# Layer 0's modulation and early-shift sums: VectorE's 32x32 block transposes and one small product each in place of ScalarE's copy and four TensorE transposes

## The chip, the core and the metric

The kernel runs on one core of a Trainium2 chip. Five engines work in parallel, each through its own instructions in program order: TensorE (PE; its weight loads are listed apart as PEld), VectorE (DVE), ScalarE (ACT), GpSimd (POOL) and SyncE (SP), whose queue issues the DMAs. The metric is the device time of one execution in microseconds (us), as the median of the runs.

## The reference

Two layers over 256 latent and 256 context tokens of width 2048. Layer 0 mixes tokens by centred pooling in four channel groups; layer 1 by neighbourhood attention. Each is followed by a gated MLP with a width-3 convolution (inner width 5504). Cut to what bears on the change:

```python
silu_c, silu_cc = jax.nn.silu(c), jax.nn.silu(c_ctx)
for i in range(DEPTH):                                  # DEPTH = 2
    ml = (silu_c @ w_mod[i] + b_mod[i]).reshape(B, 6, 1, D)     # latent: 6 chunks of D
    mc = (silu_cc @ w_mod[i] + b_mod[i]).reshape(6, 1, 1, D)    # context, same weights
    a_lat = modulate(rms_norm(h, norm1_g[i]), ml[:, 0], ml[:, 1])
    a_ctx = modulate(rms_norm(hc, norm1_g[i]), mc[0], mc[1])
    ...                                                 # i == 0: y = pool_mix(a)
    h = h + ml[:, 2] * y_lat
    h = h + ml[:, 5] * conv_ffn(modulate(rms_norm(h, norm2_g[i]), ml[:, 3], ml[:, 4]),
                                ffn_w_gate[i], ffn_w_up[i], ffn_conv_w[i], ffn_conv_b[i], ffn_w_down[i])
```

`modulate(x, shift, scale)` is `x * (1 + scale) + shift`. The context stream goes through the same steps with `mc`.

## The kernel before

Activations lie with channels on the partitions: 16 blocks of 128 channels, 256 latent and 256 context columns. Products with the large weights run as three TensorE passes over rounded high and low parts (high x high, high x low, low x high); ScalarE casts the high part of a weight tile and VectorE subtracts it to get the low part (`split`, lines 143 and 145; tiles such as `wcu_4h` and `wcu_4l`). The tiles of the high parts come from a pool of three buffers, so the cast of a new tile also waits until TensorE has read the old one.

Layer 0's modulation is 24 chunks of 512 channels: chunk 4w+g is part w of the six (shift, scale, gate, then the MLP's three) in channel group g. Generator `mod_pe` makes one chunk in 16 small TensorE products (line 193, tile `mod`), each with 32 columns of weights at one of four column positions of the array; a product is float32 and shows as two matmuls in the trace. Its result, 128 partitions by 512, holds the two streams in a few rows, and in partial sums over four row blocks. To get channels onto the partitions, ScalarE copies the PSUM bank to `modev` (line 198), TensorE transposes it in four pieces into `modt` (line 203), VectorE reduces over the row blocks (`by_row`, line 205) and adds the bias (`finish_mod`, line 181; for scales, line 183 follows). Only one PSUM bank, tag `m`, serves the `mod` tiles, so a chunk's first product waits until the chunk before it was read out.

The order of the chunks is per group g: g, 4+g, 8+g, 16+g, 12+g, then 20 to 23. `need(n)` steps this row of generators from within the code of the mixer and of `partial`.

The pooling mixer works per channel group: `mixer(g)` normalises and modulates (`py`, line 453; `pad` on ScalarE), sums windows by doubling (`ws`, line 461, VectorE), divides (`pf` on GpSimd, line 466), subtracts (line 467) and splits into high and low (`ph`), for four blocks; then a 512x512 product `pm` with the split weights `wph`, `wpl`; `gsc` and `gbi` come from the gate chunk 8+g. Group g+1's mixer is interleaved with `partial(g, ...)`, which runs the first eight column blocks of the MLP's gate and up products over group g's channels (`cg`, `cu`, lines 545 to 547) as soon as those channels are ready.

The MLP's shift term goes through the same weights: `partial` has small products `pwg` and `pwu` (line 528), also 32 columns wide, 16 times in all (four groups, two halves, gate and up). They are turned like the modulation: ScalarE's copy `peg`, `peu` (line 532), four transposes `ptg`, `ptu` (line 561), a reduce, and for g > 0 an add into `wsh` (lines 564 to 569).

Layer 1's modulation is made on VectorE instead (line 241) and already ends in a block transpose (line 251) and a product with `quad`, a matrix of ones where partition numbers agree modulo 32 (`quarter_sum`, line 165).

The order of the instructions on each engine comes from a scheduler that takes its priorities from the order of the code; `tc.high_priority()` raises what stands under it. The text of the kernel alone does not give the order.

Of the kernel before, what the change touches and what calls it, by code (L numbers as in the profile page):

```python
# [10 lines left out]
F32 = mybir.dt.float32  # L11
F32R = mybir.dt.float32r
AF = mybir.ActivationFunctionType
ALU = mybir.AluOpType
AX = mybir.AxisListType
PSUM = bass.MemoryType.PSUM

P = 128
# [39 lines left out]
def kernel(ctx: ExitStack, tc: tile.TileContext, xT, cxT, wmod, wg, wu, wd, wp,  # L58
                         wq, wv, wo, vec, cc, rope, inv, strips, out):
    nc = tc.nc  # L60
    main = ctx.enter_context(tc.tile_pool(name="main", bufs=1))
# [7 lines left out]
    def bank(tag, name):  # L69

        if tag == "d" and nbank[0] is not None:
            nbank[0] += 1
            if nbank[0] % 4 == 0:
                tag = "m"
        return pp.tile([P, 512], F32, tag=tag, bufs={"gu": 4, "d": 3, "m": 1}[tag], name=name)

    def flat(a):
        return a.rearrange("p s t -> p (s t)")
# [5 lines left out]
    def V(name):  # L84
        a, b = _OFF[name]
        return vt[:, a:b]
# [5 lines left out]
    ident = main.tile([P, P], F32, name="ident")  # L92
# [60 lines left out]
    modT = {}  # L153

    both = (0, 1)

    def by_row(ps):

        return ps.rearrange("p (i j c) -> p i c j", i=4, j=4)[:, :, 0:2, :]

    def quarter_sum(x, n, name):


        ps = bank("d", f"{name}s")
        nc.tensor.matmul(ps[:, : 16 * n].rearrange("p (k s) -> p k s", s=n), quad, x, start=True, stop=True)
        v = ps[:, : 16 * n].rearrange("p (i b s) -> p i b s", b=4, s=n)
        return [v[32 * b : 32 * b + 32, :, b, :] for b in range(4)]

    def finish_mod(l, ch, streams, src):

        mt = src[0] if len(src) == 1 else main.tile([P, 4, 2], F32, name=f"modT{l}_{ch}")
        n = len(streams)
        which, q = divmod(ch, 4)

        def dup(name, a):
            return V(name)[:, a : a + 8].rearrange("p (i s) -> p i s", s=2)[:, :, 0:n]

        bias = dup(f"bm_{l}", 8 * ch)
        for b, v in enumerate(src):
            own = slice(32 * b, 32 * b + 32) if len(src) > 1 else slice(0, P)  # L180
            nc.vector.tensor_tensor(mt[own, :, 0:n], v, bias[own], op=ALU.add)
        if which in (1, 4):
            nc.vector.scalar_tensor_tensor(mt[:, :, 0:n], mt[:, :, 0:n], 1.0, dup(f"g{1 if which == 1 else 2}_{l}", 8 * q),
                                           op0=ALU.add, op1=ALU.mult)
        modT[l, ch] = mt

    def mod_pe(l, ch, sc, pool):

        ps = bank("m", f"mod{l}_{ch}")
        for g in range(4):  # L190
            ts = load(lambda a, b: wmod[l, ch, g, :, a:b], 2048, f"wm{l}_{ch}_{g}")
            for j in range(4):
                nc.tensor.matmul(ps[32 * j : 32 * j + 32, :], sc[:, 4 * g + j, :],  # L193
                                 ts[j // 2][0][:, 512 * (j % 2) : 512 * (j % 2) + 512],
                                 start=(g == 0), stop=(g == 3), tile_position=(0, 32 * j))
            if g == 3:
                ev = pool.tile([P, 512], F32, tag="t2", name=f"modev{l}_{ch}")
                nc.scalar.copy(ev, ps)
            yield
        with tc.high_priority():  # L200
            p2 = bank("d", f"modt{l}_{ch}")
            for i in range(4):
                nc.tensor.transpose(p2[:, P * i : P * i + P], ev[:, P * i : P * i + P], ident)
        r = main.tile([P, 4, 2], F32, name=f"modT{l}_{ch}")
        nc.vector.tensor_reduce(out=r, in_=by_row(p2), axis=AX.X, op=ALU.add)
        finish_mod(l, ch, both, [r])

    def mod_pairs(todo, ring):

# [113 lines left out]
    with ExitStack() as ph0:  # L323
        p0 = ph0.enter_context(tc.tile_pool(name="p0", bufs=1, reuse_waits="tile"))
        f0 = ph0.enter_context(tc.tile_pool(name="f0", bufs=6, reuse_waits="tile"))
# [18 lines left out]
        wsh = p0.tile([P, 2, NS, 2], F32, name="wsh")  # L344
# [41 lines left out]
        with ExitStack() as phs:  # L386
# [16 lines left out]
            for j in range(2):  # L403
                t = st.tile([P, 2, WP], F32, bufs=1, name=f"pad{j}")
# [3 lines left out]
            for j in range(2):  # L408
                t = st.tile([P, 4, 32], F32, bufs=1, name=f"sh{j}")
# [100 lines left out]
            def partial(g, sh, between):  # L510

                step = 0
                for fa in range(0, NS, 4):
                    for q, (nm, wsrc) in enumerate((("g", wg), ("u", wu))):
                        ts = load(lambda a, b: wsrc[0, fa + a // 512 : fa + b // 512, :, 512 * g : 512 * g + 512]
                                  .rearrange("f p c -> p f c"), 2048, f"wc{nm}{g}_{fa}")
                        parts = split(ts, f"wc{nm}{g}_{fa}")
                        for j in range(4):
                            f = fa + j
                            between(2 * step)  # L520
                            if j == (3 if fa == 0 and q == 0 else 0):
                                need(20 * g + 21)
                                assert g in READY
                                pw = bank("d", f"pw{nm}{g}_{fa}")
                                for i in range(4):
                                    for jj, (t, n) in enumerate(ts):
                                        t3 = t.rearrange("p (f c) -> p f c", c=512)
                                        nc.tensor.matmul(pw[32 * i : 32 * i + 32, 256 * jj : 256 * jj + 256], sh[:, i, :],
                                                         t3[:, :, P * i : P * i + P], start=True, stop=True,
                                                         tile_position=(0, 32 * i))  # L530
                                ev = f0.tile([P, 512], F32, tag="t2", name=f"pe{nm}{g}_{fa}")
                                nc.scalar.copy(ev, pw)
                            if f >= NC:
                                if g == 0:
                                    HELD[f, q] = bank("gu", f"c{nm}_{f}")
                                ps = HELD[f, q]
                                first, final = g == 0, g == 3
                            else:
                                ps = bank("d", f"c{nm}{g}_{f}")
                                first = final = True  # L540
                            hi, lo = parts[j // 2]
                            for i in range(4):
                                c = 512 * (j % 2) + P * i
                                xh, xl = flat(A[4 * g + i][:, 0]), flat(A[4 * g + i][:, 1])
                                nc.tensor.matmul(ps, hi[:, c : c + P], xh, start=(first and i == 0), stop=False)
                                nc.tensor.matmul(ps, hi[:, c : c + P], xl, start=False, stop=False)
                                nc.tensor.matmul(ps, lo[:, c : c + P], xh, start=False, stop=(final and i == 3))
                                if i == 1:
                                    between(2 * step + 1)
                            step += 1  # L550
                            if f >= NC:
                                continue
                            if g == 0:
                                if q == 0:
                                    PART[f] = act_tile(f"part{f}", F32)
                                nc.scalar.copy(PART[f][:, q], ps)
                            else:
                                nc.vector.tensor_tensor(PART[f][:, q], PART[f][:, q], ps, op=ALU.add)
                        p2 = bank("d", f"pt{nm}{g}_{fa}")
                        for i in range(4):  # L560
                            nc.tensor.transpose(p2[:, P * i : P * i + P], ev[:, P * i : P * i + P], ident)
                        w_ = wsh[:, q, fa : fa + 4, :]
                        if g == 0:
                            nc.vector.tensor_reduce(out=w_, in_=by_row(p2), axis=AX.X, op=ALU.add)
                            continue
                        t_ = f0.tile([P, 512], F32, tag="t2", name=f"pu{nm}{g}_{fa}")[:, 0:8]
                        t_ = t_.rearrange("p (f s) -> p f s", s=2)
                        nc.vector.tensor_reduce(out=t_, in_=by_row(p2), axis=AX.X, op=ALU.add)
                        nc.vector.tensor_tensor(w_, w_, t_, op=ALU.add)
            lend(range(4, KT))  # L570
            mix = mixer(0)
            for n in STEPS:
# [141 lines left out]
    with ExitStack() as ph2:  # L714
# [136 lines left out]
        for j, (a, b) in enumerate(((0, 4), (4, 6), (6, 8), (8, 12), (12, 16))):  # L851
            v = hl[:, a:b, :]
# [379 lines left out]
```

## Time and profile before

| | before |
|---|---|
| median of three runs | 3102.25 us (3098.42 to 3103.55) |
| profiled execution | 3103.48 us |
| its span | 3101.7 us |
| granted TensorE clock, mean | 0.993 |
| TensorE busy | 3030.0 us (98%) |
| VectorE busy | 1932.6 us (62%) |
| ScalarE busy | 1373.2 us (44%) |
| GpSimd busy | 826.1 us (27%) |

The profiled execution is one run; 1.78 us of its time lie outside the span. The work around the change lies in about the first 475 us. Shares over the whole span are means over stages with different limits.

### The profile page before, as it was taken

What the parts mean: (1) busy time and instruction counts of PE and PEld (TensorE: products, weight loads), DVE (VectorE), ACT (ScalarE), POOL (GpSimd) and SP (SyncE); (2) the same over time, 40 slices, a digit from 0 to 9 for tenths busy, and PEclk for the clock granted to TensorE, in tenths of its full rate; (3) what the DMA queues carried; (4) which work ended last, traced back from release to release, by engine and by line L of the source; (5) the groups of instructions that cost most, each with busy time, mean ns of one, the idle gap of its engine ahead of it and who ended that gap; (6) DMA issues with size and microseconds to landing.
All of it is one profiled execution on the core that took longest, in us unless ns stands there. A gap on an engine that the chain in (4) does not pass through costs nothing.

```text
span 3101.7 us, 40819 instructions
## 1 busy us (share of the span) xinstructions
PE 3030.0 (98%) x15082; PEld 2414.3 (78%) x15082; DVE 1932.6 (62%) x2748; ACT 1373.2 (44%) x2219; POOL 826.1 (27%) x823
## 2 busy tenths in 40 slices
PE   6999899999999999999999999999999999999998
PEld 2565558888888888888888788878788888888887
DVE  4445674285765848567485665564777666666666
ACT  3333454333233332323334444343545666656665
POOL 2011213213031230302213000000002466556665
PEclk9999999999999999999999999999999999999999
DMA  9978573264846657475573333332345565555563
GB/s 376 333 271 306 177 246 102 89 217 149 251 141 206 198 162 247 133 225 171 182 226 118 102 113 106 102 114 96 111 153 179 177 196 188 192 189 185 179 195 117
DMA packets 177927, 559.70 MB, mean 180 GB/s; under 512 B 17600, under 2 KB 22208, under 8 KB 177728
## 3 DMA queue, kind: packets, MB, share of 16 engines
q1 hardware_dynamic: 177728, 557.10, 55.0%
q8 instruction: 119, 1.95, 0.3%
q14 instruction: 80, 0.66, 0.1%
HBM read 554.93 MB, written 2.10 MB: 180 GB/s over the span
## 4 chain that ended last, share of the span: by engine, by line
PE 94%; DMA 2%; DVE 2%; POOL 1%; ACT 1%; issue 0%; SPq 0%; DVEq 0%; ACTq 0%; POOLq 0%
PE g L766 5%; PE u L766 5%; PE d L657 5%; PE d L659 5%; PE d L658 5%; PE d L813 4%; PE u L631 4%; PE u L632 4%; PE u L633 4%; PE g L631 4%; PE g L633 4%; PE g L632 4%; PE mod L193 3%; PE u L769 3%; PE g L769 3%; PE d L817 2%
## 5 line engine op out<-in xcount | busy, mean ns | idle before, releaser
L670 POOL TENSOR_TENSOR hl<-hl,dy 128x256 f32<-128x256 f32 x160 | 149.0, 931 | 958.6 <-ACT dy L669 957.3
L828 POOL TENSOR_TENSOR hl<-hl,dy 128x256 f32<-128x256 f32 x320 | 331.5, 1069 | 188.4 <-ACT dy L826 186.1
L241 DVE SCALAR_TENSOR_TENSOR macc<-wm,sc,macc 128x512 f32<-128x512 f32 (+1 forms) x360 | 325.2, 935 | 68.6 <-DMA wm<-wmod 67.6
L669 ACT ACTIVATE dy<-d,modT 128x256 f32<-128x256 f32 x320 | 133.5, 470 | 196.8 <-PE d L659 195.5
L193 PE MATMUL mod<-wm,sc 128*32 128x512 f32 x768 | 134.6, 618 | 26.6 <-DMA wm<-wmod 26.5
L670 POOL TENSOR_TENSOR hc<-hc,dy 128x256 f32<-128x256 f32 x160 | 126.0, 787 | 0.0
L145 DVE TENSOR_TENSOR wd_2l<-wd,wd_2h 128x1024 fp32r<-128x1024 f32 (+1 forms) x44 | 53.9, 1229 | 112.8 <-ACT wd_2h L143 112.8
L826 ACT ACTIVATE dy<-d,modT 128x512 f32<-128x512 f32 x160 | 104.4, 683 | 42.7 <-PE d L817 41.2
L915 POOL TENSOR_TENSOR rk<-rk,rp 128x256 f32<-128x256 f32 x16 | 13.2, 826 | 365.4 <-DVE rk L914 309.8
L145 DVE TENSOR_TENSOR wd_3l<-wd,wd_3h 128x1024 fp32r<-128x1024 f32 (+1 forms) x44 | 52.0, 1202 | 80.6 <-ACT wd_3h L143 80.6
L145 DVE TENSOR_TENSOR wd_1l<-wd,wd_1h 128x1024 fp32r<-128x1024 f32 (+1 forms) x44 | 53.7, 1224 | 58.6 <-ACT wd_1h L143 58.6
L466 POOL TENSOR_TENSOR pf<-ws,inv 128x256 f32<-128x256 f32 x32 | 27.7, 886 | 222.4 <-DVE ws L461 154.7
L193 PEld LDWEIGHTS mod<-wm,sc 128*32 128x32 f32 x768 | 23.6, 110 | 81.0 <-issue 59.4
L143 ACT CAST wd_1h<-wd 128x1024 fp32r<-128x1024 f32 (+1 forms) x44 | 45.2, 1029 | 79.8 <-PE u L632 50.6
L145 DVE TENSOR_TENSOR wd_0l<-wd,wd_0h 128x1024 fp32r<-128x1024 f32 (+1 forms) x44 | 54.6, 1247 | 40.7 <-ACT wd_0h L143 40.6
L1004 ACT ACTIVATE sb<-sb,nm 128x512 f32<-128x512 f32 x64 | 46.1, 721 | 64.4 <-DVE nm L1000 63.2
L143 ACT CAST wd_0h<-wd 128x1024 fp32r<-128x1024 f32 (+1 forms) x44 | 45.3, 1031 | 57.9 <-PE u L766 29.1
L792 DVE TENSOR_TENSOR actb<-sgb,actb 128x256 fp32r<-128x256 f32 x43 | 52.3, 1216 | 27.0 <-ACT actb L791 27.0
L657 PE MATMUL d<-act,wd_2h 128*128 128x512 f32 x172 | 68.0, 395 | 0.0
L658 PE MATMUL d<-act,wd_2h 128*128 128x512 f32 x172 | 67.9, 395 | 0.0
L657 PE MATMUL d<-act,wd_3h 128*128 128x512 f32 x172 | 67.9, 395 | 0.0
L657 PE MATMUL d<-act,wd_0h 128*128 128x512 f32 x172 | 67.9, 395 | 0.0
(1752 smaller groups left out, 9286.1 us busy)
## 6 DMA issues: line engine op xcount, KB each, us to landing
wm<-wmod SPq DMA_DIRECT2D x384, 512.0 KB, 6.1
wd<-wd SPq DMA_DIRECT2D x168, 512.0 KB, 4.4
wg<-wg SPq DMA_DIRECT2D x156, 512.0 KB, 4.6
wu<-wu SPq DMA_DIRECT2D x156, 512.0 KB, 4.5
wv<-wv SPq DMA_DIRECT2D x32, 512.0 KB, 3.9
wk<-wq SPq DMA_DIRECT2D x32, 512.0 KB, 4.0
wq<-wq SPq DMA_DIRECT2D x32, 512.0 KB, 3.7
wo<-wo SPq DMA_DIRECT2D x32, 512.0 KB, 4.4
```

What stands on the lines that cost most here:

```text
L145: eng.tensor_tensor(lo[:, :n], t[:, :n], hi[:, :n].bitcast(F32), op=ALU.subtract)
L193: nc.tensor.matmul(ps[32 * j : 32 * j + 32, :], sc[:, 4 * g + j, :], ts[j // 2][0][:, 512 * (j % 2) : 512 * (j % 2) + 512], start=(g == 0) ...
L241: nc.vector.scalar_tensor_tensor(acc[s], v, sc2[:, k, s : s + 1], acc[s], op0=ALU.mult, op1=ALU.add)
L631: nc.tensor.matmul(ps, hi[:, c : c + P], xh, start=(k == 0), stop=False)
L632: nc.tensor.matmul(ps, hi[:, c : c + P], xl, start=False, stop=False)
L633: nc.tensor.matmul(ps, lo[:, c : c + P], xh, start=False, stop=(k == KT - 1))
L657: nc.tensor.matmul(ps, hi[:, o : o + P], xh, start=(i == 0), stop=False)
L658: nc.tensor.matmul(ps, hi[:, o : o + P], xl, start=False, stop=False)
L670: nc.gpsimd.tensor_tensor(h_of(s)[:, k, :], h_of(s)[:, k, :], y[:, s], op=ALU.add)
L766: nc.tensor.matmul(ps, hi[:, c : c + P], flat(B[k]), start=(k == 0), stop=False)
L769: nc.tensor.matmul(ps[:, T:], lo[:, c : c + P], B[k][:, 0], start=False, stop=(k == KT - 1))
L828: nc.gpsimd.tensor_tensor(hl[:, k, :], hl[:, k, :], y[:, q], op=ALU.add)
```

## The change

For all 24 chunks of layer 0's modulation and for the 16 shift sums, `turned` takes the place of ScalarE's copy: VectorE transposes the PSUM bank in blocks of 32x32 into a tile in SBUF. `quarter_sum` then takes the place of the four TensorE transposes and of the reduce: one float32 product of `quad` with a strided 32 columns of that tile. Its result lies in four quarters of 32 partitions, so `finish_mod` makes four adds in place of one, and a shift sum ends in four copies (g = 0) or four adds.

```diff
-    def by_row(ps):
-        return ps.rearrange("p (i j c) -> p i c j", i=4, j=4)[:, :, 0:2, :]
+    def turned(ps, pool, name):
+        t = pool.tile([P, 512], F32, tag="t2", name=name)
+        nc.vector.transpose(t, ps)
+        return t.rearrange("p (k r) -> p k r", r=32)[:, :, 0:2]
...
             if g == 3:
-                ev = pool.tile([P, 512], F32, tag="t2", name=f"modev{l}_{ch}")
-                nc.scalar.copy(ev, ps)
+                x = turned(ps, pool, f"modev{l}_{ch}")
             yield
         with tc.high_priority():
-            p2 = bank("d", f"modt{l}_{ch}")
-            for i in range(4):
-                nc.tensor.transpose(p2[:, P * i : P * i + P], ev[:, P * i : P * i + P], ident)
-        r = main.tile([P, 4, 2], F32, name=f"modT{l}_{ch}")
-        nc.vector.tensor_reduce(out=r, in_=by_row(p2), axis=AX.X, op=ALU.add)
-        finish_mod(l, ch, both, [r])
+            v = quarter_sum(x, 2, f"modt{l}_{ch}")
+        finish_mod(l, ch, both, v)
...
-                                ev = f0.tile([P, 512], F32, tag="t2", name=f"pe{nm}{g}_{fa}")
-                                nc.scalar.copy(ev, pw)
+                                x = turned(pw, f0, f"pe{nm}{g}_{fa}")
...
-                        p2 = bank("d", f"pt{nm}{g}_{fa}")
-                        for i in range(4):
-                            nc.tensor.transpose(p2[:, P * i : P * i + P], ev[:, P * i : P * i + P], ident)
-                        w_ = wsh[:, q, fa : fa + 4, :]
-                        if g == 0:
-                            nc.vector.tensor_reduce(out=w_, in_=by_row(p2), axis=AX.X, op=ALU.add)
-                            continue
-                        t_ = f0.tile([P, 512], F32, tag="t2", name=f"pu{nm}{g}_{fa}")[:, 0:8]
-                        t_ = t_.rearrange("p (f s) -> p f s", s=2)
-                        nc.vector.tensor_reduce(out=t_, in_=by_row(p2), axis=AX.X, op=ALU.add)
-                        nc.vector.tensor_tensor(w_, w_, t_, op=ALU.add)
+                        for b, v in enumerate(quarter_sum(x, 2, f"pt{nm}{g}_{fa}")):
+                            w_ = wsh[32 * b : 32 * b + 32, q, fa : fa + 4, :]
+                            if g == 0:
+                                nc.vector.tensor_copy(w_, v)
+                            else:
+                                nc.vector.tensor_tensor(w_, w_, v, op=ALU.add)
```

The change also moves instructions that it does not name. Line numbers below are each kernel's own; after the change line 193 is 195, 453 is 450, 461 is 458, 467 is 464, 470 is 467, 545 to 547 are 541 to 543, the new block transpose is line 160 and the new product line 167.

VectorE before, in the mixer of group 2, where chunk 10's result is read (`modT_10`; `wp2l` is the low part of the mixer's weights, `py`, `ws`, `pf`, `ph` are the pooling chain):

```order
L453 SCALAR_TENSOR_TENSOR py_1770<-hl,modT_6_1639,rs_194 128x256
L453 SCALAR_TENSOR_TENSOR py_1770<-hc,modT_6_1639,rs_194 128x256
L145 TENSOR_TENSOR wp2l_1863<-wp_1024_1856,wp2h_1862 128x1024
L205 TENSOR_REDUCE modT_10_1758<-modt_10_1753 128x8
L467 TENSOR_TENSOR pf_1724<-pf_1724,pad_200 128x512
L461 TENSOR_TENSOR ws_1775<-pad_198 128x2x271
L181 TENSOR_TENSOR modT_10_1758<-modT_10_1758,vt 128x8
```

VectorE after, at the same place:

```order
L458 TENSOR_TENSOR ws_1704<-ws_1704 128x2x265
L145 TENSOR_TENSOR wp2l_1844<-wp_1024_1837,wp2h_1843 128x1024
L160 STREAM_TRANSPOSE modev_10_1729<-mod_10_1627 128x512
L450 SCALAR_TENSOR_TENSOR py_1753<-hl,modT_6_1621,rs_194 128x256
L450 SCALAR_TENSOR_TENSOR py_1753<-hc,modT_6_1621,rs_194 128x256
L464 TENSOR_TENSOR pf_1708<-pf_1708,pad_200 128x512
L183 TENSOR_TENSOR modT_10_1739<-modt_10s,vt 32x8 x4
```

Before, VectorE's part in chunk 10 came after TensorE's; now its transpose comes first, one pair of `py` earlier, and behind `wp2l`.

VectorE before, in the mixer of group 3, around chunk 11:

```order
L145 TENSOR_TENSOR wp3l_2611<-wp_0_2606,wp3h_2610 128x1024
L461 TENSOR_TENSOR ws_2469<-ws_2469 128x2x257
L453 SCALAR_TENSOR_TENSOR py_2520<-hl,modT_7_2387,rs_194 128x256
L453 SCALAR_TENSOR_TENSOR py_2520<-hc,modT_7_2387,rs_194 128x256
L467 TENSOR_TENSOR pf_2474<-pf_2474,pad_200 128x512
L461 TENSOR_TENSOR ws_2525<-pad_198 128x2x271
L205 TENSOR_REDUCE modT_11_2508<-modt_11_2503 128x8
L461 TENSOR_TENSOR ws_2525<-ws_2525 128x2x269
L181 TENSOR_TENSOR modT_11_2508<-modT_11_2508,vt 128x8
L145 TENSOR_TENSOR wp3l_2615<-wp_1024_2608,wp3h_2614 128x1024
```

VectorE after, at the same place:

```order
L145 TENSOR_TENSOR wp3l_2583<-wp_1024_2576,wp3h_2582 128x1024
L458 TENSOR_TENSOR ws_2440<-ws_2440 128x2x269
L467 TENSOR_TENSOR ph_2411<-pf_2407,ph_2411 128x512
L458 TENSOR_TENSOR ws_2440<-ws_2440 128x2x265
L458 TENSOR_TENSOR ws_2440<-ws_2440 128x2x257
L160 STREAM_TRANSPOSE modev_11_2466<-mod_11_2362 128x512
L450 SCALAR_TENSOR_TENSOR py_2490<-hl,modT_7_2356,rs_194 128x256
L450 SCALAR_TENSOR_TENSOR py_2490<-hc,modT_7_2356,rs_194 128x256
```

The second half of `wp3l`, which stood behind chunk 11's add, now stands ahead of chunk 11's transpose, with four pooling steps between.

TensorE before, in group 3's early products, where chunk 3 is turned (`cg_964` and `cg_1002` are the two gate blocks that stay in PSUM over all groups, `mod_7` the scale chunk of group 3):

```order
L193 MATMUL mod_3_2140<-wm_3_3_1024_2244,sc 32x512 x2
L545 MATMUL cg_964<-Ad_2039,wcg_4h_2360 128x512
L546 MATMUL cg_964<-Ad_2039,wcg_4h_2360 128x512
L545 MATMUL cg_1002<-Ad_2039,wcg_4h_2360 128x512
L546 MATMUL cg_1002<-Ad_2039,wcg_4h_2360 128x512
L203 MATMUL modt_3_2266<-ident,modev_3_2250 128x128 x4
L193 MATMUL mod_7_2274<-wm_7_0_0_2275,sc 32x512 x2
```

TensorE after, up to the same chunk's product:

```order
L543 MATMUL cg_995<-Ad_2041,wcg_4l_2333 128x512
L541 MATMUL cg_995<-Ad_2046,wcg_4h_2332 128x512
L542 MATMUL cg_995<-Ad_2046,wcg_4h_2332 128x512
L543 MATMUL cg_995<-Ad_2046,wcg_4l_2333 128x512
L167 MATMUL modt_3s<-modev_3_2225,quad 128x32
L195 MATMUL mod_7_2248<-wm_7_0_0_2249,sc 32x512 x2
```

Before, four of the 24 products of these two gate blocks stood here, two more ahead of chunk 11's first product, and 18 between the turns of chunks 7 and 11; after, all 24 stand ahead of chunk 3's product. Six of the `cg_4` products moved ahead of chunk 7's turn as well, so that between the turns of chunks 7 and 11 TensorE has 41 large products left of 65, and seven small ones. In group 2, 17 `cg`, seven small ones and 24 `cu` lie between the turns of chunks 6 and 10, where 23 `cg` lay before.

## The prediction

> **What bounds the kernel now.** All rows are of one profiled execution. I read the page first: the busy times, and the chain of work that ended last.
>
> ```profile
> PE 3030.0 (98%) x15082; PEld 2414.3 (78%) x15082; DVE 1932.6 (62%) x2748; ACT 1373.2 (44%) x2219; POOL 826.1 (27%) x823
> PE 94%; DMA 2%; DVE 2%; POOL 1%; ACT 1%; issue 0%; SPq 0%; DVEq 0%; ACTq 0%; POOLq 0%
> ```
>
> TensorE is the bound over the whole. VectorE's 62% looks like room for 40 transposes. But the change works in the first 475 us, so I cut that stretch into windows. One of them, from the middle of group 2's mixer (columns: PE, PEld, DVE, ACT, POOL busy, granted clock, DMA share, GB/s):
>
> ```profile
> 225.00:250.00 25.00, 23.56 (x133) 14.03 (x132) 22.63 (x38) 9.18 (x16) 7.45 (x8) 1.00 0.84 295
> ```
>
> Here VectorE is busy 22.63 of 25 us, ScalarE 9.18. The change takes work from the idle engine and gives it to the full one. VectorE works in order, so a transpose starts only when the pooling steps ahead of it are done; TensorE works in order too and must pass the product that reads it. What counts is therefore where TensorE will stand and wait. The waits view has what it waited for ScalarE's copy before (total us, times, longest):
>
> ```profile
> PE modt L203 <- ACT modev L198: 7.8, 7, 1.6
> ```
>
> **TensorE's own work.** The four transposes lie between large products, or ahead of small ones:
>
> ```profile
> L203 PE MATMUL modt<-ident,modev x96: 270/272/475, 32.4 to 452.9; 128*128 128x128 f32 x96
> 219.38 0.60 PE L203 MATMUL modt<-ident,modev 128*128 128x128 f32 x4
> 219.74 0.48 PE L546 MATMUL cg<-Ad,wcg_4h 128*128 128x512 f32 x1
> 220.05 0.40 PE L547 MATMUL cg<-Ad,wcg_4l 128*128 128x512 f32 x1
> 323.71 0.60 PE L203 MATMUL modt<-ident,modev 128*128 128x128 f32 x4
> 324.24 1.07 PE L193 MATMUL mod<-wm,sc 128*32 128x512 f32 x8
> 675.43 0.30 PE L165 MATMUL modt_0s<-modr,quad 128*128 128x32 f32 x2
> 675.57 0.48 PE L631 MATMUL g<-A,wg_14h 128*128 128x512 f32 x1
> 675.88 0.40 PE L632 MATMUL g<-A,wg_14h 128*128 128x512 f32 x1
> ```
>
> Matmuls overlap, so I take the distance of the starts. From 219.38 to 220.05 pass 0.67 us, of which 0.23 are the large product's usual pitch: 0.44 for four transposes. Ahead of a small product it is 0.53 (323.71 to 324.24). Layer 1's product with `quad` has the shape that layer 0 now gets: 675.43 to 675.88 is 0.45, less 0.23 leaves 0.22. Each conversion saves 0.22 to 0.31, and 24 + 16 = 40 of them 8.8 to 12.4; I take **-10.6 us**.
>
> Some of it comes back, as the scheduler cuts the small modulation products into other runs:
>
> ```profile
> 302.64 1.92 PE L193 MATMUL mod<-wm,sc 128*32 128x512 f32 x14
> 304.49 0.51 PE L545 MATMUL cg<-Ad,wcg_4h 128*128 128x512 f32 x1
> 309.24 1.05 PE L193 MATMUL mod<-wm,sc 128*32 128x512 f32 x2
> 310.22 0.50 PE L545 MATMUL cg<-Ad,wcg_4h 128*128 128x512 f32 x1
> ```
>
> A run of 2 to 8 costs one slot, 0.98 us (309.24 to 310.22); one of 14, two slots, costs 1.85 (302.64 to 304.49). So 0.87 a slot, 0.11 a run, and 0.09 more at its entry. By the order there were 87 runs with 122 slots before, and there are 92 with 126: 4 x 0.87 + 5 x 0.20 = **+4.5**. A run that ends in a half-filled slot is the cause.
>
> **ScalarE and VectorE.** Rows for what goes, and for what the later layer has of what comes:
>
> ```profile
> L198 ACT COPY modev<-mod x24: 564/585/590, 31.7 to 448.8; 128x512 f32<-128x512 f32 x24
> L251 DVE STREAM_TRANSPOSE modu<-macc x32: 665/686/708, 663.4 to 1687.5; 128x512 f32<-128x512 f32 x32
> 677.79 0.68 DVE L181 TENSOR_TENSOR modT<-modt_0s,vt 32x8 f32<-32x8 f32 x4
> 678.50 1.23 DVE L145 TENSOR_TENSOR wu_14l<-wu,wu_14h 128x1024 fp32r<-128x1024 f32 x1
> ```
>
> ScalarE loses 40 x 0.585 = 23.4 us, worth nothing in itself: it had 9.18 of 25 us. VectorE's transpose from SBUF took 0.69; none from PSUM was traced. The nearest PSUM rows bound it: the copy's 0.585 below, and 0.69 again above (taken). Four small adds take 0.71 (677.79 to 678.50). VectorE's extra is about 40 us over 475; only what sits ahead of a waiting TensorE counts.
>
> **Group 2, chunk 10.** VectorE's rows, then TensorE's:
>
> ```profile
> 221.58 1.23 DVE L145 TENSOR_TENSOR wcu_4l<-wcu,wcu_4h 128x1024 fp32r<-128x1024 f32 x1 [5.43 <-ACT wcu_4h L143]
> 222.72 0.18 DVE L205 TENSOR_REDUCE modT<-modt 128x8 f32<-128x32 f32 x1
> ...
> 223.03 1.22 DVE L145 TENSOR_TENSOR wcu_4l<-wcu,wcu_4h 128x1024 fp32r<-128x1024 f32 x1
> ...
> 234.70 0.48 DVE L453 SCALAR_TENSOR_TENSOR py<-hl,modT,rs 128x256 f32<-128x256 f32 x1
> ...
> 235.98 1.75 DVE L145 TENSOR_TENSOR wp2l<-wp,wp2h 128x1024 fp32r<-128x1024 f32 x1
> 237.65 0.18 DVE L205 TENSOR_REDUCE modT<-modt 128x8 f32<-128x32 f32 x1
> ...
> 234.17 0.66 PE L203 MATMUL modt<-ident,modev 128*128 128x128 f32 x4 [1.44 <-ACT modev L198]
> ```
>
> From 221.58 to 237.65 VectorE runs through: 16.07 us. In the new order the transpose stands at the end of that list, less one `py` pair (235.98 - 234.70 = 1.28), with four adds for the reduce and add (0.71 for 222.72 to 223.03, +0.40), and itself 0.69: it ends at 221.58 + 16.07 - 1.28 + 0.40 + 0.69 = 237.5. TensorE reached this place at 234.17 - 1.44 = 232.7, now 232.4 with chunk 6 cheaper: a wait of 5.1 where 1.44 was, **+3.7**. If TensorE's earlier savings bring it here sooner while the load behind `wcu_4h` does not move, they are waited away as well: 18 of the 40 conversions lie ahead of this place, 18/40 of the net 10.6 - 4.5 is 2.7 us, so up to +6.4. I take **+4.5**, nearer the row's own distance.
>
> **Group 3, chunk 11.** Here nothing waited before (323.71 has no bracket):
>
> ```profile
> 304.83 0.60 PE L203 MATMUL modt<-ident,modev 128*128 128x128 f32 x4
> 323.25 0.39 PE L546 MATMUL cu<-Ad,wcu_4h 128*128 128x512 f32 x1
> ...
> 317.40 0.69 DVE L470 TENSOR_TENSOR ph<-pf,ph 128x512 fp32r<-128x512 f32 x1
> 318.00 1.46 DVE L461 TENSOR_TENSOR ws<-ws 128x538 f32<-128x538 f32 x2
> 319.38 1.22 DVE L145 TENSOR_TENSOR wp3l<-wp,wp3h 128x1024 fp32r<-128x1024 f32 x1
> 320.52 0.69 DVE L461 TENSOR_TENSOR ws<-ws 128x514 f32<-128x514 f32 x1
> ...
> 323.72 1.05 ACT L143 CAST wp3h<-wp 128x1024 fp32r<-128x1024 f32 x1 [0.64 <-PE cu L546]
> ```
>
> Turn 7 to turn 11 took TensorE 18.88 us. With 24 large products moved ahead of turn 7, 24 x 0.228 = 5.5 go, and the small products run as one: about 11.5 are left. And the last row shows a chain. The second cast `wp3h` began when the last `cu` that reads `wcu_4h` had ended (323.25 + 0.39), because that frees its buffer. In the new order `wp3l` of this cast stands ahead of chunk 11's transpose. So TensorE comes to the product just after freeing the buffer, and then waits for cast 1.05, `wp3l` 1.14 (319.38 to 320.52), three `ws` at 0.69 (318.00 to 319.38 is two), `ph` 0.60 (317.40 to 318.00) and transpose 0.69: **5.5 us**, whatever came before. Up to 7.3 if that `wp3l` is stretched like the 1.75 us one of group 2 (+0.6), ScalarE is late by a cast (+0.6), or GpSimd by as much. I take **+6.0**.
>
> **The clock.** After long waits the products run slower (the windows' columns as above):
>
> ```profile
> 383.89 1.95 PE L528 MATMUL pwu<-wcu,sh 128*32 128x256 f32 x14 [4.13 <-DMA wcu<-wu]
> ...
> 384.00:385.00 1.00, 1.00 (x11) 0.52 (x14) 0.05 (x1) 0.92 (x1) 0.00 (x0) 0.50 0.98 356
> 386.00:387.00 1.00, 1.00 (x3) 0.81 (x4) 0.18 (x1) 0.59 (x1) 0.00 (x0) 0.50 0.59 217
> 387.00:388.00 1.00, 1.00 (x5) 0.78 (x4) 0.00 (x0) 0.00 (x0) 0.00 (x0) 0.80 0.87 279
> ```
>
> After 4.13 us idle the granted clock was 0.50 until about 387.6, 3.7 us: 1.85 us lost. The 1.44 us wait of group 2 left it at 1.00 (window above). Both new waits exceed 4.13, so 2 x 1.9 = **+3.8**; 0 if neither trips it, 6.6 if the slow spell lasts nearly twice as long.
> The Trainium skill, page "TensorE: Matmul & The Clock Gate", Part 1, states that an idle window of about 3.4 us halves the clock until some 3.4 us of busy work; by that it is 1.7 a wait, +3.4 in all. The trace agrees, with its 3.7 us.
>
> **The rest.** The seven waits for the copy become waits for VectorE: 0.1 longer each by the durations, and four adds make `modT` 0.4 later for whoever needs it; an early-group transpose may sit behind a pooling step. I take **+1.5**, 0 to 4. After 475 us the order is unchanged.
>
> **Sum.** -10.6 + 4.5 + 4.5 + 6.0 + 3.8 + 1.5 = **+9.7 us**. On the profiled 3103.48 (1.78 of it outside the span) that is 3113.2; on the median, 1.23 lower, **3112**.
>
> **Rivals.** *VectorE comes in time (faster).* If the transposes at chunks 10 and 11 were done when TensorE arrives, only its own work is left: -10.6 + 4.5 = -6.1, 3096; with the 12.4 saved, -7.9, 3094. This needs VectorE some 5 us earlier at both places; from there on it decides. For it: idle gaps such as the 5.43 us at 221.58. Against: the order, and 22.63 of 25 us. The Trainium skill, "VectorE: DVE Perf Modes", rules for kernel authors, calls VectorE's transpose the fastest for 32x32 blocks; that would favour this rival, and the durations agree, but it prices no place in a queue.
> *Short waits (no change).* If chunk 10 waits only for cast 1.05, `wp2l` 1.14 and transpose 0.69, 2.9 in place of 1.44, and the clock holds: -6.1 + 1.5 + 5.5 = +0.9, 3103.
> *Contention (slower still).* With the least saving and the upper ends: -8.8 + 4.5 + 6.4 + 7.3 + 6.6 + 4 = +20, 3122. POOL's 7.45 us in the window, beside which `wp2l` took 1.75, speak for it.
>
> **Chances.** Forecast 0.47, of it 0.05 within the bound; in time 0.13, of it 0.10 faster; short waits 0.22; contention 0.18. About 0.2%, 6.2 us, can be told from no change. So faster (below 3096) 0.10, same 0.30, slower (above 3108.5) 0.60. Range 3097 to 3122: it leaves out the faster rival's better half and the worst of contention. The slower cases' own range is 3108 to 3122.
>
> **What would show it.** In the changed trace: products at `modt_10s` and `modt_11s` with idle brackets near 5 and 6 us released by VectorE, both followed by a granted clock near 0.5; about 0.22 us for a product elsewhere. If these brackets are under 2 us, the forecast is wrong, and so is its sign; if waits as long stand at other chunks, the rest was too small.

## The result, and the profile after

The change made the kernel slower: 3115.72 us as the median of six runs (3113.08 to 3117.72) against 3102.12 of the kernel before, a ratio of 1.0043 (95% interval 1.003 to 1.0056), or +13.6 us. The profiled execution took 3115.59 us, its span 3113.8.

Busy times and the chain that ended last, of the page after the change:

```profile
PE 3033.1 (97%) x15002; PEld 2409.9 (77%) x15002; DVE 1967.8 (63%) x2872; ACT 1352.0 (43%) x2179; POOL 826.4 (27%) x823
PE 89%; DVE 2%; POOL 1%; DMA 1%; ACT 1%; issue 1%; DVEq 0%; SPq 0%; POOLq 0%; ACTq 0%
```

ScalarE is 21 us lighter, VectorE 35 us heavier, and TensorE is still the bound, with less of the chain. The waits view names the places (us in total, times, longest):

```profile
PE modt_11s L167 <- DVE modev L160: 5.7, 1, 5.7
PE modt_10s L167 <- DVE modev L160: 5.1, 1, 5.1
...
PE modt_8s L167 <- DVE modev L160: 4.7, 1, 4.7
```

Three waits for VectorE's transposes, each about three times the longest wait for ScalarE's copy before (1.6) or more. The timeline around the last two, with what follows each:

```profile
243.74 0.60 PE L167 MATMUL modt_10s<-modev,quad 128*128 128x32 f32 x2 [5.09 <-DVE modev L160]
244.28 1.94 PE L195 MATMUL mod<-wm,sc 128*32 128x512 f32 x8
...
341.88 0.61 PE L167 MATMUL modt_11s<-modev,quad 128*128 128x32 f32 x2 [5.73 <-DVE modev L160]
342.42 1.94 PE L195 MATMUL mod<-wm,sc 128*32 128x512 f32 x8
```

Eight small products took 1.94 us here and 1.07 before (at 324.24): behind both waits TensorE ran at half clock. The windows show it (the last three columns are granted clock, DMA share and GB/s):

```profile
50.00:75.00 25.00, 20.28 (x71) 9.05 (x72) 11.75 (x20) 8.22 (x16) 7.19 (x8) 0.75 1.02 401
225.00:250.00 25.00, 19.91 (x97) 11.73 (x96) 20.79 (x42) 8.07 (x12) 4.04 (x5) 0.87 0.85 303
325.00:350.00 25.00, 19.27 (x98) 11.00 (x97) 23.35 (x47) 6.74 (x11) 4.30 (x6) 0.86 0.68 237
```

These three clocks were 0.86, 1.00 and 1.00 before. What stood ahead of chunk 11's transpose, on TensorE, ScalarE, GpSimd and VectorE in turn:

```profile
335.54 0.39 PE L542 MATMUL cu<-Ad,wcu_4h 128*128 128x512 f32 x1
336.00 1.04 ACT L143 CAST wp3h<-wp 128x1024 fp32r<-128x1024 f32 x1
334.38 1.65 POOL L463 TENSOR_TENSOR pf<-ws,inv 128x256 f32<-128x256 f32 x2 [58.17 <-DVE ws L458]
336.06 0.69 DVE L464 TENSOR_TENSOR pf<-pf,pad 128x512 f32<-128x512 f32 x1 [0.63 <-POOL pf L463]
336.67 0.72 DVE L458 TENSOR_TENSOR ws<-pad 128x542 f32<-128x542 f32 x1
337.31 1.22 DVE L145 TENSOR_TENSOR wp3l<-wp,wp3h 128x1024 fp32r<-128x1024 f32 x1
338.44 0.72 DVE L458 TENSOR_TENSOR ws<-ws 128x538 f32<-128x538 f32 x1
339.07 0.69 DVE L467 TENSOR_TENSOR ph<-pf,ph 128x512 fp32r<-128x512 f32 x1
339.67 1.44 DVE L458 TENSOR_TENSOR ws<-ws 128x530 f32<-128x530 f32 x2
341.02 0.71 DVE L160 STREAM_TRANSPOSE modev<-mod 128x512 f32<-128x512 f32 x1
```

The last reader of `wcu_4h` ends at 335.93, the cast starts at 336.00 and is done at 337.04. VectorE gets to `wp3l` only at 337.31, because it had waited for GpSimd's `pf` until 336.06 and had two steps ahead of `wp3l`; from 336.06 its steps follow one another to the transpose's end at 341.73. So the cast was ready 0.27 us before it was needed. The profile's chain of work that ended last (start, us, engine and work; most pieces left out) runs the same way. It does not pass through the cast, and goes back past more than 18 us of TensorE's products to a load of `wcu`:

```profile
316.46 1.02 PE mod L195 x8
317.48 5.80 DMA wcu<-wu
...
334.38 1.66 POOL pf L463 x2
...
341.11 0.64 DVE modev L160
341.88 0.39 PE modt_11s L167
```

At chunk 10 the chain is alike, from a load that starts at 219.99, again behind a run of `mod` products, to the transpose's end at 243.61.

To see where the time is (12.1 us between the two profiled spans), I sum for each kind of TensorE work the distance from a product's start to the next one's, less the idle time in between, up to 520 us of the span; the clock's row takes windows of 1 us, busy time times (1 - granted clock), up to 480 us, and lies inside the rows above it.

| us | before | after | difference |
|---|---|---|---|
| turns of the 24 chunks | 12.7 | 6.6 | -6.1 |
| turns of the 16 shift sums | 9.2 | 5.1 | -4.1 |
| small modulation products (`mod`) | 127.7 | 136.6 | +8.9 |
| small shift products (`pwg`, `pwu`) | 18.4 | 20.5 | +2.1 |
| pooling products (`pm`) | 45.3 | 47.5 | +2.2 |
| early gate and up products (`cg`, `cu`) | 191.5 | 192.6 | +1.1 |
| idle after the first product | 23.0 | 34.1 | +11.1 |
| of the work above: lost at lower clock | 4.6 | 11.7 | +7.1 |

The rows without the last one come to +15.2. The norm sums' products, which have no row, took 1.6 us less, and TensorE's first product started 0.7 us sooner; that leaves the +12.9 us by which TensorE's later products lie behind at 520 us.

### The profile page after: what moved, and what is told of

The parts are those of the page before. It is cut to its first block, busy times and chain, and to the rows that moved or that the text cites. A ratio compares the mean times of both kernels' runs of the same rounds, so it can differ in the third digit from the quotient of the medians.

```text
span 3113.8 us, 40760 instructions
## 1 busy us (share of the span) xinstructions
PE 3033.1 (97%) x15002; PEld 2409.9 (77%) x15002; DVE 1967.8 (63%) x2872; ACT 1352.0 (43%) x2179; POOL 826.4 (27%) x823
## 4 chain that ended last, share of the span: by engine, by line
PE 89%; DVE 2%; POOL 1%; DMA 1%; ACT 1%; issue 1%; DVEq 0%; SPq 0%; POOLq 0%; ACTq 0%
PE g L757 5%; PE u L757 5%; PE d L648 5%; PE d L650 5%; PE d L649 5%; PE d L804 4%; PE u L622 4%; PE u L623 4%; PE u L624 4%; PE g L622 4%; PE g L624 4%; PE g L623 4%; PE g L760 3%; PE u L760 3%; PE d L808 2%; PE mod L195 2%
## 5 line engine op out<-in xcount | busy, mean ns | idle before, releaser
L195 PE MATMUL mod<-wm,sc 128*32 128x512 f32 x768 | 143.7, 626 | 24.7 <-DMA wm<-wmod 24.6
```

## The experiments

My theory: TensorE waits where a transpose stands behind other work in VectorE's queue, and runs at half clock after it. The main rival: VectorE's added load as such. All experiments share one switch (here with the chunks of the first); each was timed 5 to 11 times, beside 18 or 27 runs of the kernel before.

```diff
+    OLD = (10, 11)
...
-                x = turned(ps, pool, f"modev{l}_{ch}")
+                if ch in OLD:
+                    ev = pool.tile([P, 512], F32, tag="t2", name=f"modev{l}_{ch}")
+                    nc.scalar.copy(ev, ps)
+                else:
+                    x = turned(ps, pool, f"modev{l}_{ch}")
...  # chunks in OLD: four transposes, tensor_reduce and one add as before the change
```

| kernel | turned the new way | median us | ratio to before (95%) |
|---|---|---|---|
| before | none | 3101.2 to 3101.8 | |
| after | all | 3115.72 | 1.0043 (1.003 to 1.0056) |
| `two_old` | all but chunks 10, 11 | 3109.03 | 1.0027 (1.0018 to 1.0037) |
| `three_old` | all but 8, 10, 11 | 3109.98 | 1.0029 (1.0018 to 1.0041) |
| `three_new` | chunks 8, 10, 11 | 3109.15 | 1.0025 (1.0015 to 1.0035) |
| `vcopy3` | all but 8, 10, 11, whose copy is VectorE's | 3117.54 | 1.0053 (1.0041 to 1.0066) |
| `shift_only` | shift sums | 3105.62 | 1.0011 (1.0002 to 1.002) |
| `mod_only` | 24 chunks | 3123.61 | 1.0068 (1.0054 to 1.0081) |
| `mod_late` | shift sums, chunks 12 to 19 | 3104.39 | 1.0008 (0.9999 to 1.0016) |
| `scales_12` | shift sums, chunks 1, 2, 5, 6 | 3106.05 | 1.0016 (1.0007 to 1.0025) |
| `keep3` | all but chunk 3 | 3115.84 | 1.0053 (1.0041 to 1.0066) |
| `only3` | chunk 3 | 3104.70 | 1.0011 (1.0002 to 1.002) |
| `keep3_8_10` | all but 3, 8, 10 | 3107.64 | 1.002 (1.0012 to 1.0029) |
| `keep_pool` | all but 0, 3, 4, 8 to 11 | 3105.95 | 1.0016 (1.0007 to 1.0025) |

**Chunks 10 and 11 the old way** (`OLD = (10, 11)`).

> The changed kernel, but chunks 10 and 11 are turned the old way (ScalarE's copy, four TensorE transposes, one reduce). Theory (TensorE waits for a transpose that stands in VectorE's queue, and then runs at half clock): the waits of 5.09 and 5.73 us at chunks 10 and 11 fall to about 1.5 and 0, the granted clock after them stays at 1.00, so -3.6 - 5.7 for the waits, -4.6 for the slow spells (about 3.0 and 1.6 us by the rows behind the two products), +0.6 for eight transposes: 3102 us. Rival A (the clock costs nothing): 3107. Rival B (VectorE's added 40 us as such, spread over all 40 conversions): 38/40 of the loss stays, 3115.

Measured 3109.03: 6.7 us of the 13.3 that the theory's terms come to, half. That rules out rival B's 3115; 3109 stands nearer to rival A's 3107 than to the theory's 3102, but the clock did cost (8.8 us lost at lower clock in all against 11.7, 3 of the 4.6 expected). The wait at chunk 10 fell to 2.50 us, not 1.5, and there is a wait at chunk 11 that the theory had at nothing, with another behind it:

```profile
335.10 0.66 PE L214 MATMUL modt<-ident,modev 128*128 128x128 f32 x4 [1.96 <-ACT modev L206]
341.25 0.50 PE L559 MATMUL cu<-Ad,wcu_4h 128*128 128x512 f32 x1 [2.31 <-DVE modT L216]
```

ScalarE's copy is late too, since the order still brings TensorE to chunk 11 early, and the next large product waits 2.31 us until VectorE's reduce frees a PSUM bank. The queue is still waited for, one step on.

**Chunks 8, 10 and 11 the old way** (`OLD = (8, 10, 11)`).

> The changed kernel, but chunks 8, 10 and 11 are turned the old way. Theory: as with two, and chunk 8's wait of 4.71 us falls to about 1.1, with about 1 us less at half clock: 3102 - 3.6 - 1 + 0.3 = 3098 us, below the 3102.1 of before, as the TensorE work saved by the other 37 conversions is left. Rival A (no clock cost): 3103.5. Rival B (VectorE's load as such): 3115.

Measured 3109.98, no better than two, against 3098 expected. The work on TensorE fell (the turns are as cheap as after, `mod` is 128.0), but idle time is 32.5 us, near the changed kernel's 34.1, and 12.7 us are lost at lower clock, more than its 11.7. The waits are 2.08, 1.44 and 2.15 us at chunks 8, 10 and 11, and others stand in new places; the largest early one is

```profile
84.19 0.50 PE L559 MATMUL cg<-Ad,wcg_0h 128*128 128x512 f32 x1 [2.49 <-ACT wcg_0h L143]
```

a wait for a cast on ScalarE. The theory names the waits of one order; another choice of chunks gives another order, with its own.

**Chunks 8, 10 and 11 alone the new way** (`OLD` holds the other 21 chunks; the shift sums as before the change).

> The kernel before, with chunks 8, 10 and 11 alone turned the new way. By the order TensorE comes to chunk 11 as before, with the 18 cg products still between the turns of chunks 7 and 11. Theory: waits of about 4.7 us at chunk 8 (+3.6) with 1 us more at half clock, about 2.7 at chunk 10 (235.4 for the transpose's end against TensorE's 232.7; +1.2), none at chunk 11 (VectorE came to that place at 321.1, TensorE at 323.7); -0.9 for three conversions: 3102.1 + 5 = 3107 us. Rival C (a transpose in VectorE's queue costs 5 us at each of these three places wherever the cg products stand): 3102.1 + 3.6 + 3.7 + 5.7 + 5 = 3120. Rival B (VectorE's load): 3103.

Measured 3109.15, nearest to the theory's 3107 in the number, and well off rival B's 3103. The rows:

```profile
57.09 0.64 PE L172 MATMUL modt_8s<-modev,quad 128*128 128x32 f32 x2 [3.98 <-DVE modev L165]
...
236.30 0.41 PE L172 MATMUL modt_10s<-modev,quad 128*128 128x32 f32 x2 [1.98 <-DVE modev L165]
...
328.01 0.30 PE L172 MATMUL modt_11s<-modev,quad 128*128 128x32 f32 x2
```

3.98 and 1.98 us where 4.7 and 2.7 were expected, and none at chunk 11: with the `cg` products back in their place, VectorE's transpose (325.43 to 326.14 in this run) is done before TensorE comes. The same conversion is free or brings a wait of 5.7 us by what else stands between. The sum is less good than the number: these two waits grew by 3.4 us where 4.8 were expected, but idle time rose by 7.2 us in all, and the lower clock cost 3.5 us more than before where 1 was expected.

**VectorE's copy in place of the transpose.**

```diff
+    OLD = (8, 10, 11)
...
-                    nc.scalar.copy(ev, ps)
+                    nc.vector.tensor_copy(ev, ps)
```

> Chunks 8, 10 and 11 keep the old four transposes, but their copy is made by VectorE; it stands where the transposes stand in the changed kernel. The other 37 conversions are new. Theory (the place in VectorE's queue counts, not what is done there): waits of 4.6, 5.0 and 5.6 us at chunks 8, 10 and 11 and the slow spells behind them stay, so 3115.7 + 0.9 for twelve transposes = 3116 us. Rival D (block transpose and product with quad are themselves the cost): as with ScalarE's copy, 3098.

Measured 3117.54, near the theory's 3116 (rival D: 3098). One row stands for the three waits of 4.27, 4.83 and 5.52 us; the view ends at 243 us and so counts three of its four transposes:

```profile
242.40 0.87 PE L214 MATMUL modt<-ident,modev 128*128 128x128 f32 x3 [4.83 <-DVE modev L206]
```

The only difference to `three_old` in the code is the engine of three copies, and it is worth 7.6 us (medians 3117.54 and 3109.98); idle time is 38.6 us against 32.5. Between the turns of chunks 7 and 11 TensorE has 41 large products in both, as in the changed kernel. At these three chunks it is the place in VectorE's queue that costs, not the block transpose nor the product. The 8.8 us by which `three_old` is still behind the kernel before are another matter. The Trainium skill, "Perfetto Trace Analysis", Optimizing Scalar/DVE Operations, states that with a saturated DVE some work may be better given to Scalar; these two runs agree, in the stretches where VectorE is full.

**The shift sums alone** (`OLD` holds all chunks).

> Only the 16 shift sums are turned the new way; the 24 modulation chunks keep the copy and four transposes. By the order the cg products stand at chunk 11 as before, no transpose of a shift sum stands ahead of a product that TensorE is early for, and the small modulation products fall into 86 runs with 120 slots (87 and 122 before). Theory (place in the queue counts): no new wait, so only TensorE's own work: -16 x 0.27 = -4.3 and -1.9 for two slots and a run: 3102 - 6 = 3096 us. Rival B (VectorE's load as such, by its share of the conversions): 3102 + 0.4 x 13.6 = 3107.

Measured 3105.62, slower than before by 4 us, not faster by 6. Rival B's 3107 lies within the interval, so this run alone does not rule it out. TensorE's own saving came (turns of the shift sums 9.2 to 4.3 us, `mod` 127.7 to 126.6), but idle time rose from 23.0 to 28.3 us, in pieces of 0.3 to 2.1 us:

```profile
324.69 0.55 PE L214 MATMUL modt<-ident,modev 128*128 128x128 f32 x3 [1.44 <-ACT modev L206]
367.23 1.12 PE L314 MATMUL n2b<-n2d,ones 128*128 128x512 f32 x2 [1.57 <-DVE n2d L312]
```

The first row's view ends at 325 us, so it too counts three of four transposes. Neither place waited as long before (0 and 0.53). My "no new wait" failed: the first wait is at chunk 11, which was not even converted.

**The 24 chunks alone** (all chunks new, the shift sums as before the change).

> Only the 24 modulation chunks are turned the new way; the shift sums are as before. By the order all 24 cg products again stand ahead of chunk 3's product, the transposes of chunks 8, 10 and 11 stand behind the pooling steps as in the changed kernel, and the small products fall into 96 runs with 129 slots. Theory: waits of about 4, 5 and 5.5 us at chunks 8, 10 and 11 (+13 less the 2.5 of before) and 7 us at half clock, -24 x 0.27 = -6.5, +8 for seven slots and nine runs: 3102 + 19 = 3121 us. Rival B: 3102 + 0.6 x 13.6 = 3110.

Measured 3123.61, near the theory's 3121, and the worst of all. The waits are 3.76, 4.40 and 5.94 us at chunks 8, 10 and 11; `mod` takes 136.9 us (127.7 before) in its 96 runs. (The profiled execution took 3120.13.) With all chunks converted, the shift sums on top take 8 us off, though alone they cost 4: the effects of the conversions don't add up.

**Late chunks, and quiet chunks** (`OLD` = 0 to 11 and 20 to 23; `OLD` = all but 1, 2, 5, 6).

> The shift sums and the chunks 12 to 19 are turned the new way; chunks 0 to 11 and 20 to 23 keep the copy and four transposes. By the order the cg products stay at chunk 11 as before, and the small products fall into 83 runs with 117 slots. Theory: the transposes of chunks 16 to 19 stand behind VectorE's norm sums and may hold TensorE about 1 us each (1.02 us at chunk 19 was seen with three chunks turned the old way); -24 x 0.27 = -6.5, -5.2 for five slots and four runs, +2 to +4: 3094 us, faster than both kernels. Rival B (VectorE's load): 3102 + 0.6 x 13.6 = 3110.

> The shift sums and the chunks 1, 2, 5 and 6 (shift and scale of groups 1 and 2) are turned the new way, the other 20 chunks the old way. Here VectorE has little queued when these chunks end (5.35 of 25 us busy between 200 and 225 us before), and the cg products stay at chunk 11; 87 runs with 121 slots. Theory: no wait of note, -20 x 0.27 = -5.4 and -0.9 for one slot: 3096 us. Rival B: 3102 + 0.5 x 13.6 = 3109.

Measured 3104.39 and 3106.05, against 3094 and 3096. Rival B's 3110 for `mod_late` lies outside the interval; its 3109 for `scales_12` lies just inside, so that run does not rule it out. Over all runs rival B's figures are outside the intervals of `two_old`, `three_new`, `mod_only` and `mod_late`. `mod_late` saved 6.5 us of TensorE's work by the table's sums and had 10.7 us more idle time; `scales_12` 2.5 and 5.7. The savings are real and are waited away.

**Chunk 3 the old way, and chunk 3 alone the new way** (`OLD = (3,)`; and all but 3, with the shift sums as before the change).

> The changed kernel, but chunk 3 alone is turned the old way. By the order the cg products then come back between the turns of chunks 7 and 11 (58 large products there; 41 in the changed kernel), and the second wp3l goes behind chunk 11's transpose; chunk 11 itself is still turned the new way, chunks 8 and 10 too. Theory (the wait at chunk 11 comes of chunk 3's conversion, which lets the scheduler move the cg products): the wait of 5.73 us at chunk 11 falls below 0.5 and the 2.0 us at half clock behind it go, +0.3 for the transposes: 3115.7 - 7.4 = 3108 us. Rival E (the wait belongs to chunk 11's own place in VectorE's queue, with either order): it stays above 3 us, 3114 to 3116.

> The kernel before, with chunk 3 alone turned the new way; by the order the cg products move ahead of its product as in the changed kernel, 47 large products are left between the turns of chunks 7 and 11, and chunk 11 keeps ScalarE's copy. 86 runs with 122 slots. Theory: chunk 3 itself waits for nothing, but TensorE comes early to chunk 11 and waits there for the copy (1.96 us, and 2.31 us more at the next large product for a PSUM bank, when chunks 10 and 11 alone were turned the old way): 3102 + 3.5 = 3105 us. Rival F (a moved product costs nothing where the copy is ScalarE's): 3101.

`only3` came at 3104.70 (expected 3105): chunk 3 waits for nothing itself, yet in its profile TensorE waits 1.44 us for the copy at chunk 11 and 1.07 us behind it, as the order moves. `keep3` came at 3115.84, not 3108. Its profiled execution is the slowest of five (3121.90; the others took 3114.88 to 3120.11), so its rows are one case and not the median:

```profile
337.08 0.38 PE L172 MATMUL modt_11s<-modev,quad 128*128 128x32 f32 x2
...
367.84 0.73 PE L559 MATMUL cg<-Ad,wcg_0h 128*128 128x512 f32 x2 [1.52 <-ACT Ad L517]
369.07 0.65 PE L560 MATMUL cg<-Ad,wcg_0h 128*128 128x512 f32 x1 [0.49 <-DVE Ad L518]
...
386.05 1.83 PE L314 MATMUL n2b<-n2d,ones 128*128 128x512 f32 x2 [1.69 <-DVE n2d L312]
```

The wait at chunk 11 is gone, as the theory said and rival E did not. But 20 to 50 us later the work behind it, pooling products, chunk 19's transpose, norm sums and the next `cg`, makes TensorE wait 0.5 to 1.7 us at five places (three of them shown), and the clock halves there (below). In this execution idle time is 32.9 us, 1.2 less than in the changed kernel, and 14.2 us are lost at lower clock, 2.5 more. By the medians nothing was gained (3115.84 and 3115.72).

**The two mixes** (`OLD = (3, 8, 10)`; `OLD = (0, 3, 4, 8, 9, 10, 11)`).

> Chunks 3, 8 and 10 are turned the old way, the other 37 conversions are new; 86 runs with 124 slots. Theory: no wait at chunk 11, 1.5 to 2.5 us at chunk 10 and 2.1 at chunk 8 for the copy, 2.5 us at the first cg product and 1.7 us at half clock behind it as when 8, 10 and 11 were turned the old way, 2 to 4 us of short waits elsewhere: 3102 - 10 + 1.7 + 1 + 2.5 + 1.7 + 0.5 + 3 = 3102 us. Rival (no new short waits): 3094.

> Chunks 0, 3, 4, 8, 9, 10 and 11 (those next to the pooling chain, and chunk 3) are turned the old way, the other 17 chunks and the 16 shift sums the new way; 86 runs with 122 slots, as many slots as before. Theory: 33 x 0.26 = -8.6 of TensorE's work, +4 to +6 of short waits as with the shift sums alone (their idle time was 5.3 us above before's): 3102 - 8.6 + 5 = 3098 us, a little faster than both. Rival (the short waits grow with the number of conversions, as the gains do): 3102 to 3105.

Measured 3107.64 and 3105.95 against 3102 and 3098: better than the full change, not better than before. Both have 7 to 8 us more idle time than before (30.7 and 29.9). No version tried beats the kernel before; `mod_late` cannot be told from it.

## Why the prediction was right, point by point

Forecast +9.7 us, measured +13.6.

- **TensorE's own work, -10.6.** Measured -10.2, in the table's first two rows; the turns at lower clock, about 0.9 us of them, are also in the clock's row.
- **Cut runs, +4.5.** `mod` rose by 8.9; about 4.0 of that lie in the clock's row (the slow rows quoted above, 1.94 for 1.07, among them), which leaves about 5.
- **Chunk 10, a wait of 5.1.** Measured 5.09, so +3.65 and not the +4.5 taken. The fear was that TensorE comes sooner while the load behind `wcu_4h` doesn't move. But the load follows a run of `mod` products on TensorE (it starts at 213.55 us before and at 219.99 after, by the chain), so the two moved together, by some 6 us. From the load's first use to the transpose's end VectorE took 15.93 us, and the forecast's terms come to 15.88. That is closer than its reasons: VectorE stood in two waits, 1.21 us in all, that the prediction didn't have, and its last `wp2l` took 1.22 us where 1.75 was taken over. So the last tenths are luck; the 5 us are not.

```profile
227.67 1.23 DVE L145 TENSOR_TENSOR wcu_4l<-wcu,wcu_4h 128x1024 fp32r<-128x1024 f32 x1 [4.05 <-ACT wcu_4h L143]
...
232.92 0.72 DVE L458 TENSOR_TENSOR ws<-pad 128x542 f32<-128x542 f32 x1 [0.58 <-ACT pad L452]
...
238.53 0.69 DVE L464 TENSOR_TENSOR pf<-pf,pad 128x512 f32<-128x512 f32 x1 [0.63 <-POOL pf L463]
...
241.75 1.22 DVE L145 TENSOR_TENSOR wp2l<-wp,wp2h 128x1024 fp32r<-128x1024 f32 x1
242.89 0.71 DVE L160 STREAM_TRANSPOSE modev<-mod 128x512 f32<-128x512 f32 x1
```

- **Chunk 11, 5.5 us "whatever came before".** Measured 5.73, and the steps from `wp3l` on are the ones named: three `ws`, `ph`, transpose. But the freed buffer and its cast did not set the start, since the cast was ready 0.27 us early. VectorE's own queue did, behind GpSimd's `pf` and the load, as at chunk 10; the prediction had GpSimd only in its upper bound. The two paths ended almost together, and that the forecast is within a quarter of a microsecond is in part luck.
- **The clock, +3.8.** This is the term that was too small: +7.1. Behind chunks 10 and 11 it lost 3.25 and 2.03 us, not 1.9 each, 1.1 us more than before around chunk 8 and 0.8 more behind the load near 402 us. The spell that the prediction measured, 3.7 us near 384, had begun within the wait, at 380.57, and lasted 6.83 us; so did the spells at chunks 10 and 11. What a spell costs is the part of it in which TensorE works, and that was nearly all of it at chunk 10:

```profile
380.60:387.35 6.75, 3.46 (x18) 1.92 (x19) 1.98 (x2) 1.63 (x2) 0.00 (x0) 0.50 0.88 296
...
243.60:250.30 6.70, 6.56 (x33) 2.27 (x33) 6.51 (x18) 1.53 (x3) 1.07 (x2) 0.50 0.72 215
339.20:345.90 6.70, 4.02 (x24) 1.84 (x28) 6.55 (x15) 1.64 (x3) 1.59 (x2) 0.50 0.08 11
```

The first row is of the kernel before, the others of the changed one.

- **The rest, +1.5.** Idle time rose by 11.1 in all, 3.65 and 5.73 of it at chunks 10 and 11, so +1.7 is left. That the sum is right is luck: chunk 8 alone rose from 1.08 to 4.71, which the prediction did not price, and other waits fell. By the prediction's own sign (waits as long at other chunks) this term was too small. VectorE's rows, and TensorE's, at chunk 8:

```profile
55.90 1.12 DVE L467 TENSOR_TENSOR ph<-pf,ph 128x512 fp32r<-128x512 f32 x1
57.05 0.72 DVE L160 STREAM_TRANSPOSE modev<-mod 128x512 f32<-128x512 f32 x1
57.91 0.61 PE L167 MATMUL modt_8s<-modev,quad 128*128 128x32 f32 x2 [4.71 <-DVE modev L160]
```

It is the same mechanism in group 0: the transpose stands behind the pooling's last steps.

- **The sum.** As measured, -10.2 + 5.0 + 3.65 + 5.73 + 7.1 + 1.7 is +13.0, where TensorE lies 12.9 us behind at 520 us, the spans differ by 12.1 and the medians by 13.6. The terms do not cover everything: other products took about 3.0 us more at full clock (`pm`, `pwg`, `pwu`, `cg` and `cu`), which the norm sums, the earlier start and the 0.9 us counted twice nearly cancel.
- **The rival "in time"** had its condition right and its price wrong. Where VectorE came in time (chunk 11 in `three_new` and in `keep3`) the wait was gone, but 3096 was never reached. The prediction took the waits as additive; the runs showed that taking one away hands part of it, in `keep3` all of it, to the next place. *Short waits* failed on the wait at chunk 10 (5.09 us, not 2.9) and on the clock, which did not hold; *contention* failed on its upper ends for the waits (+3.65 and 5.73, not 6.4 and 7.3), but the clock's 7.1 us are above even its 6.6.

What stays open is what holds this stage. TensorE's savings of 2.5 to 6.5 us became idle time in `shift_only`, `scales_12` and `mod_late` alike. In the changed kernel the chain ahead of chunks 10 and 11 leaves TensorE for 24 us each time, through a load of `wcu` and VectorE's steps behind it. A kernel with these loads started earlier would test whether they hold the stage; it wasn't tried, nor an order with the transposes put first in VectorE's queue. And no run explains one by one the 8.8 us by which `three_old` stays behind the kernel before, with the three long waits gone.

## What to carry to other kernels

Price a moved step by the queue that it joins: read from the new order what stands ahead of it, and add up those rows until the waiting engine's place. A gain on the bounding engine counts only if its next wait doesn't grow by as much; and an edit that touches a scheduler's order should be costed at the places that it never names, since converting one chunk (`only3`) moved 20 large products and brought a wait to another chunk. A gap on TensorE can cost more than its length, through the clock behind it (here 2.0 to 3.3 us behind waits of 5 to 6).

## What the runs showed of the hardware

- VectorE's block transpose from PSUM took 0.717 us, from SBUF 0.686 (medians; 128x512 float32), and its plain copy from PSUM 0.685 (three copies of `vcopy3`).

```profile
L160 DVE STREAM_TRANSPOSE modev<-mod x24: 702/717/719, 29.0 to 464.8; 128x512 f32<-128x512 f32 x24
```

- The clock's records show a grid. In all 14 traces every spell at half clock before 485 us lasts 3.41 us or two, three or four times that, and all spells of one execution start on one grid of 3.41 us. Divided on that grid from 25 to 485 us, the traces have 1779 stretches at full clock. The 56 that were followed by half clock had TensorE busy for 55% or less; of the 1723 others four had it busy for less than 50%, none for less than 42%. By these figures it is the idle share of a stretch that counts, so the same wait can cost a spell or none: `only3` and `shift_only` both wait 1.96 us at chunk 10, and 3.41 us at half clock follow in the first, none in the second, where a boundary of the grid (at 232.22 us) falls within the wait.

- The clock can halve without a long gap. In `keep3` no wait between 362 and 370 us exceeds 1.52 us, and yet:

```profile
368.00:370.00 2.00, 1.51 (x5) 0.88 (x6) 1.88 (x7) 2.00 (x7) 0.00 (x0) 0.82 1.03 410
370.00:374.00 4.00, 4.00 (x15) 3.08 (x15) 1.71 (x5) 0.80 (x3) 0.00 (x0) 0.50 0.61 217
374.00:378.00 4.00, 4.00 (x13) 2.40 (x9) 0.00 (x0) 0.00 (x0) 0.00 (x0) 0.50 0.34 124
```

It stayed at 0.50 for over 8 us although TensorE was busy throughout; 5.1 us were lost there. `mod_late`, with waits of 1.52 and 0.48 us near 356, ran at half clock for 3.41 us there. The Trainium skill, "TensorE: Matmul & The Clock Gate", A second HAM failure mode: psum-queue depth-cycling, tells of frequent short idle gaps that make the clock swing (HAM is its name for what sets the clock); the short waits here agree with it. The Trainium skill, "TensorE: Matmul & The Clock Gate", Part 1, states that the clock is full again after some 3.4 us of sustained busy work. Here that does not hold: the spell took more than twice that, with small products and sums among the work.
